# Where the gating branch and the front of the first head pair stand in a two-layer hybrid RWKV-7 / gMLP step

## The chip, the core and the metric

The kernel runs on one core of a Trainium2 chip. The metric is the time of one execution on the device, in microseconds: 3382.55, the median of three runs (3381.95 to 3396.24). TensorE multiplies matrices, VectorE and ScalarE work on elements, GpSimd (POOL in the profile) takes some element work, and SyncE (SP) issues all transfers, in order, from one queue. Every engine takes its own instructions in the order in which the program has them.

## What is computed

Two layers work on 640 tokens: 128 of a context and 512 of a latent grid, each with its own modulation. Of one layer, cut to what matters:

```python
z = h @ p['w_in'][l]                       # h: the normed, modulated input
z_rwkv, z_u, z_v, z_ga, z_gb = jnp.split(z, ...)
z_rwkv = z_rwkv + mu_shift * (shift_fn(z_rwkv) - z_rwkv)
y_a, S_fin = rwkv_branch(z_rwkv, S0, p, l)     # r, k, v, decay and a from lora; recurrence over tokens
# gating branch
u = jax.nn.gelu(z_u); v = jax.nn.gelu(z_v)
v = (v - mu) * lax.rsqrt(var + EPS) * p['ln_v_g'][l]
s = jnp.einsum('hpq,bnqhc->bnphc', p['w_s'][l], vc) + b_s     # mixes the tokens of a chunk of 128
y_b = (u * s) @ p['w_branch_b'][l]
mixed = (sigmoid(z_ga) * y_a + sigmoid(z_gb) * y_b) @ p['w_out'][l]
x = x + g1 * mixed                         # then a feed-forward block, gated by g2
```

The recurrence has 16 heads in two directions, `S = S * w + (S @ -kk) b^T + v k^T` and `y = S r`. `mod = silu(cond) @ w_ada` gives the shifts, scales and gates (48 columns of 128 channels a layer).

## The kernel before

Activations stand channel-major, 128 channels by 640 tokens. A product with fp32 weights is three passes of a split into `hi` and `lo`; a **dense block** (`dense`) makes 128 output channels: two loads of weights (`load_w`: `raw` by SP, `hi` on ScalarE, `lo` on VectorE, or by turns on GpSimd where `engs` says so) and 48 matmuls of 320 columns (line 111).

A layer runs in these stages:

- `n1`: the norm and the three lora blocks; their results are shifted by `shift_mix` (a copy to `zraw`, six transfers into the one tile `zs`, a mix on VectorE).
- `p1`, **the gating branch**, in a pool of its own: four token-major quarters of `z_v` (line 491), 40 lora units (line 463) that write the recurrence's inputs to `ld` in HBM, eight channel-major dense blocks of `z_u` (line 505, gelu, kept in `uts`), and `spatial` (line 443), which mixes tokens per head with weights and biases loaded whole at the start. In layer 0 the 32 late modulation columns (`mod_col`, line 168: a load of 512 KB and two VectorE reductions) stand between the dense blocks.
- `rw`, **the recurrence**, pair by pair of heads. `krv_block` makes k, r and v of a pair. `front(i)` prepares pair i: the normed key (`kksq` with Ln and Exp), for each direction the decays' running sums and their exponentials (`cum`, `E`), scaled copies `LA` and `BK`, Gram matmuls `g` (line 644), transposes, and a substitution of 30 steps on VectorE (lines 676 and 678). `back(i)` runs ten steps that depend on each other: matmuls on the state `SV`, a copy to `psb` on ScalarE, matmuls, copies back to `SV` on ScalarE and VectorE, sums on VectorE; then a group norm with Ln and Exp.
- The loop over pairs writes `back(i)` and `front(i+1)` interleaved, with the k, r, v blocks of the next pairs and **gate blocks** (the 16 dense blocks of `z_ga` and `z_gb`, spilled to HBM in `gd`) as fillers. The table `SP` says how many: `g0` within the front of pair 0, `gn[i]` around the end of pair i. `front(0)` runs ahead of the loop with only k, r, v of pairs 0 and 1 and a few gate blocks beside it.
- Then `branch_b`, which loads u * s from `bd`, and `p3` and `ff`, which do the rest.

A scheduler turns this into one fixed order per engine; `front` is written under a raised priority (`F`: 200), `back` under none. `pre` loads a ScalarE table that has Ln and Exp both, once, where the `rw` pool opens; `lnexp` asks only that an instruction stands behind it.

Of the kernel before, what the change touches and what calls it, by code (L numbers as in the profile page):

```python
# [6 lines left out]
F32 = mybir.dt.float32  # L7
# [27 lines left out]
SP = {'n': (3, 2, 1, 2, 2, 1, 0, 0, 3, 1), 'v': 1, 'k': 4, 'r': 7, 'kk': 7, 'F': 200, 'B': None, 't': 10, 'g0': 2, 'gn': (2, 2, 2, 1, 2, 2, 2, 1)}  # L35
# [6 lines left out]
def emit(tc, I, O, depth=DEPTH, mark=lambda s: None):  # L42
    nc = tc.nc
    ctx = ExitStack()
    with ctx:
# [117 lines left out]
        def mod_col(l, j, scr):  # L163
            wt = scr.tile([128, DM], F32, tag="wada", name="wada", bufs=2)
# [117 lines left out]
        yd = dram.tile([NK, 128, T], F32, name="yd")  # L282
        bvd = dram.tile([NPAIR, 128, T], F32, name="bvd")
# [23 lines left out]
        for l in range(depth):  # L307
# [73 lines left out]
            with tc.tile_pool(name=f"com{l}", bufs=1) as com:  # L381
# [10 lines left out]
                mark("p1")  # L392
                with tc.tile_pool(name=f"p1_{l}", bufs=1) as p1:
                    lah = p1.tile([128, 3, T], F32R, tag="lah", name="lah")
                    lal = p1.tile([128, 3, T], F32R, tag="lal", name="lal")
                    late = iter(range(16, 48 if l == 0 else 16))
                    if l == 0:
                        silu_c(p1)

                    def mod_some(n):  # L400
                        for _, j in zip(range(n), late):
                            mod_col(0, j, p1)

                    for j in range(3):
                        mod_some(0)
                        if l == 0:
                            ps = zps[j]
                        elif j < 2:
                            if j == 0:
                                pss = dense_pair(wsrc(I["win"][l, 24]), wsrc(I["win"][l, 25]), hh, hl)  # L410
                            ps = pss[j]
                        else:
                            ps = dense(I["win"][l, 24 + j], hh, hl)
                        t = p1.tile([128, T], F32, tag="pt", name="lz", bufs=4)
                        shift_mix(ps, 24 + j, t, l, com, cnt)
                        if j == 0:
                            nc.scalar.activation(t, t, AF.Tanh)
                        elif j == 2:
                            nc.scalar.activation(t, t, AF.Tanh, scale=0.5)
                            nc.vector.tensor_scalar(t, t, 0.5, 0.5, ALU.mult, ALU.add)  # L420
                        split(lah[:, j], lal[:, j], t)
                    stat = p1.tile([128, 5, 4], F32, tag="stat", name="stat")
                    vts = [p1.tile([128, DM], F32, tag=f"v{tk}", name=f"v{tk}") for tk in range(5)]
                    uts = p1.tile([128, NK, T], F32, tag="u", name="u")
                    bs_bc = p1.tile([128, NK, 128], F32, tag="bsb", name="bsb")
                    nc.sync.dma_start(bs_bc, I["bs"][l:l + 1].to_broadcast([128, NK, 128]))
                    wst = p1.tile([128, NK, 128], F32, tag="wst", name="wst")
                    nc.sync.dma_start(wst, I["wsT"][l])
                    turn = [0]

                    def halves_ps():
                        turn[0] += 1
                        if turn[0] % 2:
                            t = dense_ps()
                            return [t[:, n] for n in range(2)]
                        tag = ("g", "pu")[turn[0] // 2 % 2]
                        return [psr.tile([128, 512], F32, tag=tag, name="hps") for _ in range(2)]

                    def spatial(h):
                        ps = halves_ps()  # L440
                        for tk in range(5):
                            o = ps[tk // 4][:, (tk % 4) * 128:(tk % 4) * 128 + 128]
                            nc.tensor.matmul(o, vts[tk][:, h * 128:(h + 1) * 128], wst[:, h, :], start=True, stop=True)
                        st = p1.tile([128, T], F32, tag="st", name="st", bufs=3)
                        bsv = bs_bc[:, h, :].unsqueeze(1)
                        nc.vector.scalar_tensor_tensor(st[:, 0:512].rearrange("p (a t) -> p a t", a=4), ps[0].rearrange("p (a t) -> p a t", a=4),
                                                       P[:, LVG + h:LVG + h + 1], bsv.to_broadcast([128, 4, 128]), ALU.mult, ALU.add)
# [28 lines left out]
                    def lora(n):  # L476
                        for _ in range(n):
                            if next(units, 0) == 0:
                                break
# [598 lines left out]
```

## Time and profile before

| | us |
|---|---|
| median of three runs | 3382.55 |
| the profiled execution | 3388.05 |
| its span | 3386.3 |
| TensorE busy (matmuls / weight loads) | 3159.4 / 2862.3 |
| VectorE, ScalarE, GpSimd busy | 2145.6, 1511.6, 612.4 |

Times of the profile are from the span's start. "Busy" of TensorE counts a matmul until its modelled end, so matmuls that wait out their latency count too. The granted clock is a share of 2.4 GHz; 0.5 is the lower of its two levels, 1.2 GHz, and what lies between is a stretch with both. The program has no stage marks; the stretches below are cut at the first evacuation of the lora blocks (72.9 and 1742 us), near the end of the gating branch (262 and 1945), and at the first and last `psb` of a layer.

### The profile page before, as it was taken

Reading aid. Unit: us, or ns where it says so; the run is one execution under the profiler, and the core shown is the slowest. Engines: PE = TensorE matmul, PEld = TensorE weight load, DVE = VectorE, ACT = ScalarE, POOL = GpSimd, SP = SyncE. Lnnn points to the kernel's source line nnn. Section 1 sums busy time; section 2 is a strip of 40 time slices with the busy share of each in tenths; the row PEclk is TensorE's granted clock in tenths of the full one; section 3 lists DMA queues with packets and bytes.
Section 4 is the critical chain, followed back from the end, with each engine's and each line's share of the span. In section 5 each row is a group of like instructions: output and inputs, shape, how many; then the busy total and the mean of one; then the engine's idle time right before and its main releaser. Section 6 shows DMA issues by size and latency. Waiting matters only on the chain.

```text
span 3386.3 us, 66312 instructions
## 1 busy us (share of the span) xinstructions
PE 3159.4 (93%) x26160; PEld 2862.3 (85%) x26160; DVE 2145.6 (63%) x4147; ACT 1511.6 (45%) x3268; POOL 612.4 (18%) x616
## 2 busy tenths in 40 slices
PE   7998899999999999999989979999999999999998
PEld 7897677777778989999989967777777789899998
DVE  7777778887785469933353487788787735532234
ACT  5444445554445354224254434445544543541432
POOL 3004333333231000000000133333323210000000
PEclk8998889998899999999999989899889999999999
DMA  6683112221224536622344522122222245222223
GB/s 210 220 291 102 56 61 72 77 74 61 66 77 138 199 104 205 216 83 75 99 135 139 188 75 66 56 73 77 68 68 72 86 137 184 84 76 75 75 75 106
DMA packets 215671, 372.73 MB, mean 110 GB/s; under 512 B 63680, under 2 KB 72000, under 8 KB 215360
## 3 DMA queue, kind: packets, MB, share of 16 engines
q1 hardware_dynamic: 215360, 368.49, 33.8%
q8 instruction: 206, 3.38, 0.4%
q14 instruction: 105, 0.86, 0.1%
HBM read 288.41 MB, written 63.31 MB: 104 GB/s over the span
## 4 chain that ended last, share of the span: by engine, by line
PE 65%; DVE 18%; DMA 5%; issue 5%; ACT 4%; POOL 3%; SPq 1%; DVEq 0%; ACTq 0%; POOLq 0%
PE dps L111 40%; PE g L644 4%; DMA wada<-in_wada 3%; PE dps L256 3%; PE dps L491 2%; DVE X L678 2%; DVE D L676 2%; PE pu L776 2%; DVE wjunk L168 2%; PE pu L757 2%; PE pu L789 1%; PE pu L795 1%; PE pu L751 1%; DVE lo L103 1%; POOL BK L625 1%
## 5 line engine op out<-in xcount | busy, mean ns | idle before, releaser
L101 ACT ACTIVATE hi<-raw 128x512 fp32r<-128x512 f32 x630 | 397.2, 632 | 1025.6 <-PE dps L111 864.0
L103 DVE TENSOR_TENSOR lo<-raw,hi 128x512 fp32r<-128x512 f32 x550 | 392.1, 714 | 545.9 <-ACT hi L101 526.7
L111 PE MATMUL dps<-ah,hi 128*128 128x320 f32 x2768 | 686.9, 324 | 8.4 <-ACT up L468 5.4
L111 PE MATMUL dps<-ah,lo 128*128 128x320 f32 x2768 | 674.3, 321 | 14.5 <-DVE lo L103 14.5
L111 PE MATMUL dps<-al,hi 128*128 128x320 f32 x2768 | 674.9, 321 | 0.0
L111 PEld LDWEIGHTS dps<-ah,lo 128*128 128x128 f32 x2768 | 474.4, 193 | 29.5 <-DVE lo L103 16.5
L111 PEld LDWEIGHTS dps<-ah,hi 128*128 128x128 f32 x2768 | 474.2, 192 | 28.2 <-ACT up L468 6.0
L111 PEld LDWEIGHTS dps<-al,hi 128*128 128x128 f32 x2768 | 473.9, 192 | 12.7 <-issue 0.8
L168 DVE CUSTOM_DVE_ANT_0 wjunk<-wada,sc 128x1024 f32<-128x1024 f32 x176 | 220.9, 1255 | 33.2 <-DMA wada<-in_wada 30.9
L785 POOL TENSOR_TENSOR sw<-SV,wc 64x128 f32<-64x128 f32 x288 | 150.7, 523 | 439.0 <-DVE SV L803 422.5
L644 PE MATMUL g<-LA,BK 64*128 64x128 f32 x1280 | 193.6, 332 | 32.9 <-DVE LA L656 15.9
L103 POOL TENSOR_TENSOR lo<-raw,hi 128x512 fp32r<-128x512 f32 x80 | 123.2, 1540 | 543.6 <-ACT hi L101 491.8
L644 PEld LDWEIGHTS g<-LA,BK 64*128 64x128 f32 x1280 | 162.0, 226 | 64.6 <-issue 22.2
L111 PE MATMUL dps<-fh,lo 128*128 128x320 f32 x896 | 205.5, 311 | 6.2 <-DVE lo L103 6.0
L111 PE MATMUL dps<-fh,hi 128*128 128x320 f32 x896 | 204.7, 310 | 0.0
L111 PE MATMUL dps<-fl,hi 128*128 128x320 f32 x896 | 204.5, 309 | 0.0
L676 DVE TENSOR_TENSOR D<-AA,X 128x30 f32<-128x30 f32 (+14 forms) x480 | 178.1, 371 | 21.6 <-POOL X L671 11.7
L678 DVE TENSOR_TENSOR X<-X,D 128x30 f32<-128x30 f32 (+14 forms) x480 | 179.9, 375 | 11.3
L249 POOL TENSOR_TENSOR al<-nt,ah 128x320 fp32r<-128x320 f32 x24 | 25.2, 1053 | 728.1 <-ACT ah L248 727.0
L111 PEld LDWEIGHTS dps<-fh,lo 128*128 128x128 f32 x896 | 150.0, 188 | 7.9 <-DVE lo L103 7.8
L625 POOL TENSOR_TENSOR BK<-ta,cum 64x640 f32<-64x640 f32 x64 | 125.8, 1966 | 141.4 <-DVE ta L616 116.3
L111 PEld LDWEIGHTS dps<-fh,hi 128*128 128x128 f32 x896 | 150.3, 188 | 0.0
(293 smaller groups left out, 5798.1 us busy)
## 6 DMA issues: line engine op xcount, KB each, us to landing
raw<-in_w SPq DMA_DIRECT2D x280, 256.0 KB, 2.6
raw<-in_win SPq DMA_DIRECT2D x234, 256.0 KB, 2.7
wada<-in_wada SPq DMA_DIRECT2D x88, 512.0 KB, 4.1
ld<-up SPq DMA_DIRECT2D x80, 320.0 KB, 3.6
th<-ld SPq DMA_DIRECT2D x32, 320.0 KB, 2.9
ta<-ld SPq DMA_DIRECT2D x32, 320.0 KB, 3.0
gd<-spill SPq DMA_DIRECT2D x32, 320.0 KB, 2.3
raw<-in_wo SPq DMA_DIRECT2D x40, 256.0 KB, 2.6
```

What stands on the lines that cost most here:

```text
L101: nc.scalar.activation(hi, raw, AF.Copy)
L103: (eng or nc.vector).tensor_tensor(lo, raw, hi.bitcast(F32), ALU.subtract)
L111: nc.tensor.matmul(ps[:, n, 0:HT], w[:, k * 128:(k + 1) * 128], xk[:, n * HT:(n + 1) * HT], start=(first and k == 0 and j == 0), stop=(las ...
L168: nc.vector.tensor_tensor_reduce(junk, wt, sc_cur[0][:, v, :], 1.0, 0.0, ALU.mult, ALU.add, mods[l][:, j, v:v + 1])
L256: nc.tensor.matmul(ps[:, n, 0:HT], w[:, k * 128:(k + 1) * 128], x[:, 4 * kb + k, hs(n)], start=(kb == 0 and k == 0 and j == 0), stop=(kb = ...
L491: nc.tensor.matmul(o, x[:, k, tk * 128:(tk + 1) * 128], w[:, kk * 256:(kk + 1) * 256], start=(k == 0 and j == 0 and tk % 2 == 0), stop=(k ...
L625: nc.gpsimd.tensor_tensor(b[s, c, 1 - h, :], rt[s], e[s], ALU.mult)
L644: nc.tensor.matmul(gs[h][:, c - c0, :], b[s, c, :, :].rearrange("p x t -> p (x t)"), la[s, c, h:h + 2, :].rearrange("p x t -> p (x t)"), s ...
L676: nc.vector.tensor_tensor(t3, AA[:, s + 1:32, s:s + 1].to_broadcast([128, n, s]), X[:, s:s + 1, 0:s].to_broadcast([128, n, s]), ALU.mult)
L678: nc.vector.tensor_tensor(X[:, s + 1:32, 0:s], X[:, s + 1:32, 0:s], t3, ALU.add)
L757: nc.tensor.matmul(pu[s, d, 3, :], SV[:, us[d], h, :], GR[d][:, cs[d], h, :], start=False, stop=True, skip_group_check=True)
L785: nc.gpsimd.tensor_tensor(sw[s], SV[s, both, h, :], wcu[s, both].unsqueeze(2).to_broadcast([64, 2, L]), ALU.mult)
```

## The change

- The pool `rw` now opens ahead of the gating branch, and so `pre` and the fronts stand ahead of it too; the tiles of odd pairs (`LA2`, `TT1` and their like) move to a pool `rwb` that takes the gating branch's room after it.
- k, r and v of pair 0 come right behind the lora inputs; half the lora units follow, and then the steps of `front(0)` are written between the quarters of `z_v`, the remaining lora units and `spatial`.
- The eight `z_u` blocks become fillers like the gate blocks: stored raw to `zud` in HBM, read back in pair 7, where gelu and the product with s are taken (`branch_b_prep`). `gn` grows from 14 to 22 fillers. `spatial` stores s alone.
- `spatial` loads its weights and bias head by head into tiles of two buffers. Lora weights are loaded half by half across the three kinds.
- The 32 modulation columns of layer 0 move to the odd steps of the pairs, with one buffer for their load.
- The scratch of dynamic transfers is made smaller (2048 bytes), which is SBUF room.

```diff
-SP = {..., 'g0': 2, 'gn': (2, 2, 2, 1, 2, 2, 2, 1)}
+SP = {..., 'g0': 2, 'gn': (2, 3, 3, 3, 3, 3, 3, 2)}
...
+                            pool = odd[0] if name in ("LA2", "LA3", "BK2", "BK3", "GR2", "GR3", "TT1") else rw
...
-                    gates = [(x, m) for x in range(2) for m in range(8)]
+                    fillers = [(27 + m, zud[m]) for m in range(8)] + [(43 + 8 * x + m, gd[x, m]) for x in range(2) for m in range(8)]
...
-                    wst = p1.tile([128, NK, 128], F32, tag="wst", name="wst")
-                    nc.sync.dma_start(wst, I["wsT"][l])
...
+                        krv(0, 0, 1, 2)
...
+                        def spatial(h):
+                            ws = p1.tile([128, 128], F32, tag="wst", name="wst", bufs=2)
+                            nc.sync.dma_start(ws, I["wsT"][l, :, h])
+                            bs = p1.tile([128, 128], F32, tag="bsb", name="bsb", bufs=2)
...
+                        lora(20)
+                        run(0, 5)
+                        for q in range(4):
...
+                            lora(5)
+                            run(0, 3)
...
+                        krv(1, 0, 1)
+                        for h in range(NK):
+                            run(0, 2)
+                            spatial(h)
+                        run(0)
...
-                        for m in range(NK):
+                    def branch_b_prep(m):
+                            bh, bl = bb["h"], bb["l"]
                             t = tmp("bs", "ta", 2)
                             nc.sync.dma_start(t, bd[m])
+                            u = ftmp("u")
+                            nc.sync.dma_start(u, zud[m])
+                            nc.scalar.activation(u, u, AF.Gelu_apprx_tanh)
+                            nc.vector.tensor_tensor(t, t, u, ALU.mult)
                             split(bh[m], bl[m], t)
...
+                        for i in range(NPAIR):
...
+                                if step % 2:
+                                    mod_some(1)
+                                if i == NPAIR - 1:
+                                    if step == 0:
+                                        branch_b_tiles()
+                                    if step < NK:
+                                        branch_b_prep(step)
```

On TensorE, where the first Gram matmuls of pair 0's front (`g`) stand: before, between dense blocks (`dps` from `ah`, `al`) behind the gating branch.

```order
L111 MATMUL dps<-ah,lo 128x320 x2
L111 MATMUL dps<-ah,hi 128x320 x2
L111 MATMUL dps<-al,hi 128x320 x2
L644 MATMUL g<-LA_2793,BK_2794 128x128 x8
L111 MATMUL dps<-ah,lo 128x320 x2
L111 MATMUL dps<-ah,hi 128x320 x2
L111 MATMUL dps<-al,hi 128x320 x2
L111 MATMUL dps<-ah,lo 128x320 x2
```

There pair 0's front has only dense blocks beside it. In the changed program, still on TensorE:

```order
L833 MATMUL dps<-lo,ah 128x256
L833 MATMUL dps<-hi,al 128x256
L833 MATMUL dps<-hi,ah 128x256
L518 MATMUL g<-LA_1148,BK_1149 128x128 x8
L833 MATMUL dps<-hi,ah 128x256
L833 MATMUL dps<-lo,ah 128x256
L833 MATMUL dps<-hi,al 128x256
L833 MATMUL dps<-lo,ah 128x256
L833 MATMUL dps<-hi,al 128x256
```

They stand now between token-major matmuls of `z_v` (line 833), inside the gating branch.

On ScalarE, in the loop's first pairs, the end of the key's norm of a later pair (`kksq`), between copies of the recurrence (`psb`, `SV`). Before:

```order
L587 ACTIVATE kksq<-k,par_163 128x640
L790 ACTIVATE SV<-pu 64x2x64
L101 ACTIVATE hi<-raw 128x512
L293 ACTIVATE zraw<-dps 128x640
L553 ACTIVATE kksq<-pg,c_e_98 128x320
L294 ACTIVATE r<-dps,dpar_165 128x640
L553 ACTIVATE kksq<-pg,c_e_98 128x320
L553 ACTIVATE kksq<-kksq 128x640
L780 ACTIVATE psb<-pu 128x128
L790 ACTIVATE SV<-pu 64x2x64
```

No table load stands there. In the changed program, at the same place:

```order
L461 ACTIVATE kksq<-k,par_164 128x640
L295 ACTIVATE r<-dps,dpar_166 128x640
L654 ACTIVATE psb<-pu 128x128
L664 ACTIVATE SV<-pu 64x2x64
L427 ACT_TABLE_LOAD
L427 ACTIVATE kksq<-pg,c_e_98 128x320 x2
L427 ACT_TABLE_LOAD
L427 ACTIVATE kksq<-kksq 128x640
L101 ACTIVATE hi<-raw 128x512
L654 ACTIVATE psb<-pu 128x128
```

A table load stands ahead of the Ln (`kksq` from `pg`) and another ahead of the Exp; the group norm's Ln and Exp have the same two.

On VectorE, in the substitution of a pair (`D`, `X`) beside the recurrence of the pair before (`SV`). Before:

```order
L678 TENSOR_TENSOR X<-X,D 128x24x7
L676 TENSOR_TENSOR D<-AA,X 128x184
L678 TENSOR_TENSOR X<-X,D 128x23x8
L791 COPY SV<-pu 64x2x64
L676 TENSOR_TENSOR D<-AA,X 128x198
L678 TENSOR_TENSOR X<-X,D 128x22x9
L803 TENSOR_TENSOR SV<-pu,sw 64x2x64
L676 TENSOR_TENSOR D<-AA,X 128x210
L803 TENSOR_TENSOR SV<-pu,sw 64x2x64
```

The substitution shares the queue with the recurrence alone there. In layer 0 of the changed program, the same place (the rows named ISA are a modulation column's reduction and its read):

```order
L638 TENSOR_TENSOR YD<-pu,YD 128x64
L552 TENSOR_TENSOR X<-X,D 128x12x19
L638 TENSOR_TENSOR YD<-pu,YD 128x64
L550 TENSOR_TENSOR D<-AA,X 128x220
L665 COPY SV<-pu 64x2x64
L552 TENSOR_TENSOR X<-X,D 128x11x20
L168 ISA wjunk,mod_171<-wada,sc 128x1024
L168 ISA mod_171 128x1
L550 TENSOR_TENSOR D<-AA,X 128x210
L677 TENSOR_TENSOR SV<-pu,sw 64x2x64
```

One reduction after the other stands between two steps of the substitution and ahead of a sum into `SV`.

## Rows read from the trace of the kernel before

**Rows 1.** Windows by stage: A:B length, busy us of each engine (instructions), PEclk, DMA share, GB/s

```profile
core 0: us, PE busy (x) PEld busy (x) DVE busy (x) ACT busy (x) POOL busy (x), PEclk, DMA share, GB/s
72.90:262.00 189.10, 176.87 (x1285) 170.37 (x1286) 137.87 (x232) 89.50 (x180) 6.79 (x13) 0.98 0.76 252
262.00:378.90 116.90, 88.86 (x683) 80.04 (x682) 93.90 (x149) 53.59 (x119) 45.29 (x29) 0.82 0.27 82
378.90:1074.30 695.40, 649.82 (x6742) 529.74 (x6741) 536.12 (x1181) 342.26 (x909) 226.57 (x240) 0.92 0.24 75
1074.30:1170.00 95.70, 95.28 (x652) 93.28 (x651) 43.59 (x69) 40.16 (x62) 0.00 (x0) 1.00 0.59 197
1742.00:1945.00 203.00, 197.60 (x1438) 192.13 (x1437) 73.42 (x114) 97.57 (x189) 11.04 (x16) 0.98 0.47 161
1945.00:2046.10 101.10, 73.74 (x588) 65.55 (x589) 82.66 (x137) 44.86 (x105) 40.84 (x26) 0.80 0.25 78
2046.10:2743.80 697.70, 651.47 (x6743) 530.94 (x6743) 537.56 (x1181) 342.48 (x909) 223.96 (x240) 0.92 0.24 75
```

**Rows 2.** Tile `psb`: ns min/median/max, first and last start in us

```profile
L780 ACT ACTIVATE psb<-pu x160: 250/278/297, 378.9 to 2743.8; 128x128 f32<-128x128 f32 x160
```

**Rows 3.** Windows of pairs of layer 0, first `psb` to next pair's first

```profile
656.30:740.00 83.70, 80.50 (x889) 64.69 (x888) 69.27 (x159) 45.30 (x122) 27.20 (x30) 0.98 0.24 72
740.00:855.00 115.00, 102.33 (x958) 85.22 (x959) 91.03 (x182) 51.98 (x136) 40.25 (x38) 0.84 0.22 70
...
1036.30:1074.30 38.00, 38.00 (x453) 29.91 (x453) 21.02 (x49) 18.75 (x47) 8.47 (x14) 1.00 0.53 168
```

**Rows 4.** Windows: between pairs 0 and 1; steps of pair 3; between pairs 3 and 4

```profile
431.10:465.10 34.00, 30.51 (x343) 26.87 (x344) 31.34 (x49) 19.75 (x41) 12.16 (x8) 0.90 0.20 61
656.30:721.30 65.00, 62.77 (x616) 50.11 (x617) 54.89 (x140) 29.58 (x89) 23.92 (x27) 0.97 0.22 68
721.30:740.00 18.70, 17.73 (x277) 14.59 (x275) 14.38 (x20) 15.72 (x34) 3.28 (x3) 1.00 0.29 87
```

**Rows 5.** Windows of 5 us between the last step of pair 0 and pair 1

```profile
445.00:450.00 5.00, 1.66 (x53) 1.39 (x53) 5.00 (x6) 2.95 (x5) 0.89 (x2) 0.83 0.30 117
450.00:455.00 5.00, 5.00 (x99) 4.61 (x97) 3.51 (x4) 2.63 (x6) 3.17 (x2) 0.50 0.17 56
...
460.00:465.00 5.00, 4.89 (x42) 3.50 (x42) 5.00 (x5) 4.82 (x13) 3.86 (x2) 1.00 0.27 86
```

**Rows 6.** Window of 50 us in layer 0's feed-forward, dense blocks alone

```profile
1450.00:1500.00 50.00, 50.00 (x343) 50.00 (x342) 13.01 (x24) 10.94 (x17) 0.00 (x0) 1.00 0.25 77
```

**Rows 7.** Groups by line: count | busy us, mean ns | idle before it and what ended it

```profile
L101 ACT ACTIVATE hi<-raw 128x512 fp32r<-128x512 f32 x630 | 397.2, 632 | 1025.6 <-PE dps L111 864.0 <-PE dps L491 48.3 <-PE dps L256 46.9
...
L168 DVE CUSTOM_DVE_ANT_0 wjunk<-wada,sc 128x1024 f32<-128x1024 f32 x176 | 220.9, 1255 | 33.2 <-DMA wada<-in_wada 30.9
...
L678 DVE TENSOR_TENSOR X<-X,D 128x30 f32<-128x30 f32 (+14 forms) x480 | 179.9, 375 | 11.3
L676 DVE TENSOR_TENSOR D<-AA,X 128x30 f32<-128x30 f32 (+14 forms) x480 | 178.1, 371 | 21.6 <-POOL X L671 11.7
...
L692 DVE STREAM_TRANSPOSE XT<-X 128x1024 f32<-128x1024 f32 x16 | 32.2, 2011 | 0.3
...
L168 DVE DVE_READ_ACCUMULATOR2_ANT mod<- 128x1 f32 x176 | 14.4, 82 | 0.0
```

**Rows 8.** Timeline of ScalarE behind pair 7: start, us taken, instruction [idle before]

```profile
1079.49 0.74 ACT L820 ACTIVATE YD<-yc 128x640 f32<-128x640 f32 x1 [1.56 <-DVE yc L818]
1080.24 1.28 ACT L553 ACT_TABLE_LOAD   x1
1081.54 0.95 ACT L553 ACTIVATE YD<-pg,c_gn 128x320 f32<-128x320 f32 x2
```

**Rows 9.** Tile `st`, ns min/median/max; transfers, KB each and median us to landing

```profile
L446 DVE SCALAR_TENSOR_TENSOR st<-dps,par,bsb x8: 744/747/753, 183.7 to 1914.0; 128x512 f32<-128x512 f32 x8
...
bd<-st SPq DMA_DIRECT2D x16, 320.0 KB, 2.7
```

More of the change, by code (lines that the diff above doesn't have):

```diff
@@ L161, in mod_setup, with mod_col @@
             mods[l] = G([128, 48, 2], f"mod{l}")
-        def mod_col(l, j, scr):
-            wt = scr.tile([128, DM], F32, tag="wada", name="wada", bufs=2)
+        def mod_col(l, j, scr, bufs=2):
+            wt = scr.tile([128, DM], F32, tag="wada", name="wada", bufs=bufs)
             nc.sync.dma_start(wt, I["wada"][l, j])
@@ L563, in krv_block, with spill_block @@
                         shift_mix(ps, blk, out, l, com, cnt)
-                    def gate_block(x, m):
-                        ps = dense(I["win"][l, 43 + 8 * x + m], hh, hl, engs=(None, nc.gpsimd))
+                    def spill_block(blk, dst):
+                        ps = dense(I["win"][l, blk], hh, hl, engs=(None, nc.gpsimd))
                         t = ftmp("spill")
                         nc.scalar.activation(pv(t), ps[:, :, 0:HT], AF.Copy)
-                        nc.sync.dma_start(gd[x, m], t)
+                        nc.sync.dma_start(dst, t)
                     def ch(t):
@@ L854, in gate @@
                         nonlocal gi
-                        for _ in range(min(n, len(gates) - gi)):
+                        for _ in range(min(n, len(fillers) - gi)):
                             mark("gate")
-                            gate_block(*gates[gi])
+                            spill_block(*fillers[gi])
                             gi += 1
@@ L868, in branch_b, with branch_b_tiles @@
+                    bb = {}
+                    def branch_b_tiles():
                         sp = []
@@ new lines, in emit, with mod_some @@
+                    with tc.tile_pool(name=f"rwb{l}", bufs=1) as rwb:
+                        odd[0] = rwb
+                        late = iter(range(16, 48 if l == 0 else 16))
+                        if l == 0:
+                            silu_c(rwb)
+                        def mod_some(n):
+                            for _, j in zip(range(n), late):
+                                mod_col(0, j, rwb, 1)
+                        b = back(0)
+                        adv(b, "B", 0)
+                        gate(SP["g0"])
+                        run(1, 5)
+                        for i in range(NPAIR):
+                            ng = SP["gn"][i]
+                            for step in range(10):
+                                adv(b, "B", i)
+                                run(i + 1, SP["n"][step])
+                                if step % 2:
[5 more added lines that the diff above has]
+                                        branch_b_prep(step)
+                                if step == SP["v"]:
+                                    krv(i + 1, 2)
+                                if step == SP["k"]:
+                                    krv(i + 2, 0)
+                                if step == SP["r"]:
+                                    krv(i + 2, 1)
+                                if step == SP["kk"]:
+                                    run(i + 2, 1)
+                            gate(ng if i == NPAIR - 1 else min(ng, 1))
+                            if i == NPAIR - 1:
+                                if l == 0:
+                                    mod_late(0)
+                                ya = new_acts()
+                                for j in range(NPAIR - 1):
+                                    t = ftmp("ya")
+                                    nc.sync.dma_start(t, yd[j])
+                                    split(ya[0][:, j], ya[1][:, j], t)
+                            drain(b, "B", i)
+                            if i == NPAIR - 1:
+                                branch_b()
+                            gate(ng - 1)
+                            run(i + 1)
+                            if i + 1 < NPAIR:
+                                b = back(i + 1)
+                                adv(b, "B", i + 1)
+                            run(i + 2, 4)
```

264 lines of the change are left out of this document (100 added, 164 removed).

## The prediction

> **What bounds the kernel now.** I read the stretches of the program first: for each layer the gating branch, the front of pair 0 that stands alone behind it, the loop over the eight pairs, and what follows [rows 1]. The loop's ends are the first and the last `psb` of a layer [rows 2]. Layer 0's gating branch takes 189.1 us with TensorE busy for 176.9; then the front of pair 0 takes 116.9 us with only 88.9 busy, at a granted clock of 0.82; layer 1 repeats this with 203.0 (197.6) and 101.1 (73.7, clock 0.80). So 40 us of layer 0 and 33 us of layer 1 are idle TensorE ahead of the loop, most of it in pair 0's front, a chain on VectorE that has too little beside it. In the loop TensorE looks full (649.8 of 695.4 us), yet weight loads are busy for only 529.7 [rows 1]: a small matmul of the recurrence counts as busy while it waits out its latency. VectorE is at 536 of 695. No engine is the bound there: it is a chain through TensorE, ScalarE and VectorE, each taking its queue in order. Its pace shows in the pairs: the last pair, with no front beside it, takes 38.0 us for its ten steps, where others take 84 to 115 us each [rows 3]; the mean over seven pairs is (1036.3 - 378.9) / 7 = 93.9 us.
>
> The sum is made on the profiled execution, 3388.05 us, 5.5 above the median of the runs, 3382.55; at the end the 5.5 comes off.
>
> **Term 1: ahead of the loop.** A dense block is 48 matmuls; where nothing else runs, 343 of them take 50 us [rows 6], 0.146 us each, 7.0 us a block. Counted in the two programs' orders, 17 blocks besides the token-major half and the lora units stand ahead of the loop before, and 7 after: ten blocks, 70 us a layer, leave. TensorE's busy time there is 176.9 + 88.9 = 265.8 us in layer 0; without the ten it is 195.8, and if the two fronts of work really overlap, that is nearly all that is left. Two new waits come. First, pair 0's substitution now runs beside the token-major blocks, which need their `lo` halves from the same VectorE queue: before the last three of these, eleven substitution steps (0.371 + 0.375 us each [rows 7]) and two transposes (2.0 us each [rows 7]) stand in a row, some 12 us, against a few us of matmuls ready; I take 12 us. Second, `spatial` loses its preloaded weights and biases to pairs of small tiles: every two heads wait for VectorE's two `st` (0.75 us each for the larger part [rows 9]), for a transfer (2.7 us to landing for the nearest, `bd` [rows 9]) and an issue queue in order; about 6 us for 2 us of matmuls, four times, so 15 us. Against that, the 0.82 means that about 42 us of 117 ran at the lower clock (1.2 GHz), which can lose 21; with TensorE kept busy I take 15 back. Layer 0: 306.0 becomes 195.8 + 27 - 15 = 208; layer 1: 304.1 becomes 271.3 - 70 + 12 = 213. **Gain 98 + 91 = 189 us.** Ends: 140, if only the blocks leave and all the idle time stays, and some 215.
>
> **Term 2: the same blocks in the loop.** Between the first step of pair 0 and that of pair 7 there are 398 more dense matmuls in layer 0 and 386 in layer 1: 784 x 0.146 = 114 us. What is paid? In the changed order a middle pair has 162 to 165 of them inside its steps and 110 to 124 between its last step and the next pair's first. Pairs with 151 to 158 inside exist already: pair 3 takes 65.0 us for its steps, and 18.7 us to the next pair with 42 matmuls there [rows 4]. Between pairs 0 and 1 stand 105, and that takes 34.0 us, of which 3.3 are idle and 5 at half the clock [rows 4, 5]; twenty more would fill those first. So a pair becomes 66 + 34 = 100 us; with the shorter pairs of the changed order (251, 279 and 197 matmuls: about 90, 99, 85) seven pairs are 674 us in place of 657: **+17 a layer, 34 in all.** Ends: 114, and below zero, since the loop's clock of 0.92 [rows 1] stands for about 110 us per layer at half rate (pair 4: 0.84 and 115 us [rows 3]). Another 143 matmuls land behind pair 7, where TensorE is busy for 95.3 of 95.7 us [rows 1]: **+21**, in full. Their transfers cost nothing: what `hi` waits for is TensorE (864 of 1025.6 us), not its `raw` [rows 7]. The second path of `zu` through HBM, and gelu and product in pair 7, lie in the emptiest pair (VectorE 21.0 of 38.0 [rows 3]).
>
> The Trainium skill, Perfetto Trace Analysis, Identifying the Most-Contended Engine, says matmul busy time is a poor measure of headroom, and weight-load busy time a good one. By matmul busy time the loop has 46 us of room per layer and a rule of thumb would charge most of the 114 (the sum below would become +36); by weight-load time it has 166 and all would fit (the sum -78). The pairs in the trace lie nearer to the second.
>
> **Term 3: table loads, which the diff doesn't show.** `pre` loads the table with both Ln and Exp once; before, it stands behind the gating branch. Now tanh and gelu of that branch run after it, so the order has a load ahead of each Ln and each Exp group: four per pair, 60 in the two loops. One takes 1.28 us, and the next instruction starts 1.30 us after it, as the end of layer 0 already shows [rows 8]: 78 us of ScalarE. Two of the four stand in the last steps, between copies of the recurrence (`psb`, `SV`); two among the copies that open the next pair, where ScalarE is already busy for 4.8 of 5 us [rows 5]. I take half, **+39**; ends 10 and 78.
>
> The Trainium skill, ScalarE: Activation LUTs, What ACT_TABLE_LOAD costs, adds a drain of about 1.38 us to each switch. By it the 60 would be 160 us, and half of that would take the sum to -3. The trace shows no such drain: the load starts at the end of the instruction ahead of it [rows 8].
>
> **Term 4: the modulation columns of layer 0.** Thirty-two of them, each two reductions of 1.255 us and two reads of 0.082 [rows 7], go from the gating branch (where TensorE was near full in any case, so nothing is won there) to the steps of pairs 0 to 6: 64 x 1.337 = 86 us of VectorE, ten reductions per pair. About three of ten stand where VectorE waits; the others lie between substitution steps and the recurrence's `SV` copies and sums. Pair 3 has VectorE busy for 69.3 of 83.7 us [rows 3]; 13.4 more would nearly fill it. I take 60%, **+51**; ends 20 and 86. The next column's load waits on SP for the one buffer; behind it queue weight blocks, which have slack [rows 7], and the shifts. I charge nothing more, and it would be part of the 86.
>
> **Sum:** -189 + 34 + 21 + 39 + 51 = -44. 3388 - 44 = 3344; on the median, **3339 us**.
>
> **The rivals.** *Slower: the recurrence's chain pays every insertion.* Place: steps 0 to 9 of each pair, on the queues of ScalarE and VectorE. Loads and columns in full are 78 + 86 = 164 in place of 90: -189 + 34 + 21 + 164 = +30, 3413 us. For it: both queues are in order and the chain goes through both. Against it: neither is full (ScalarE 342, VectorE 536 of 695 [rows 1]). It decides from 134 of the 164 on. *Faster still: the fill keeps the clock.* Blocks in the loop cost nothing and 30 us of half-rate time come back: -108, 3275 us. For it: the low clock follows slices in which TensorE idled (1.66 of 5 us busy, then 0.50 [rows 5]). Against it: the waits that idle TensorE between a pair's scaling on VectorE and its Gram matmuls stay. *It doesn't do what it says: pair 0's front and the branch take turns.* The order puts front matmuls between the branch's, but in order on one queue each can wait for the other's VectorE work; then term 1 is 140 and the sum +5, 3388 us.
>
> **How the numbers follow.** Forecast 0.5, slower chain 0.2, kept clock 0.15, taking turns 0.15. The ends of the terms around the forecast give about 60 us down and 75 up; with the rivals the range is 3265 to 3415. A measurement can tell about 0.5% (17 us) from no change, so the marks are 3366 and 3399. Faster: most of the forecast, all of the kept clock and a little of the third: 0.63. Same: 0.16. Slower: 0.21.
>
> **What would show it.** From the first evacuation of the lora inputs to the first `psb`: 208 and 213 us; over 230 says that they took turns. Layer 1's loop, which has no columns: about 735 us; near 700 says that the blocks were free, over 770 that they and the loads were paid. Layer 0's loop less layer 1's: about 50 us is the columns' price. The page should show some 90 table loads. The prediction is wrong if layer 0's loop passes 860 us, or if layer 1's does not grow.

## The result and the profile after

The changed kernel takes 3586.89 us, the median of four runs (3573.73 to 3597.73), against 3382.25 for the kernel before: 1.059 times as long (95% interval 1.055 to 1.064). The forecast was 3339 us, with 3265 to 3415 as its range. The profiled execution took 3588.89 us; its span is 3587.1.

The stages of the changed kernel, cut as in [rows 1] (length, busy us of each engine with instructions, granted clock, share of the transfers):

```profile
72.80:334.30 261.50, 220.48 (x1478) 197.95 (x1478) 128.83 (x217) 127.47 (x271) 35.90 (x36) 0.84 0.38 128
334.30:1133.30 799.00, 733.65 (x7162) 602.57 (x7159) 634.75 (x1332) 396.15 (x967) 253.66 (x253) 0.91 0.31 97
1133.30:1230.00 96.70, 96.70 (x666) 95.34 (x663) 43.36 (x68) 42.36 (x66) 0.00 (x0) 1.00 0.64 212
1810.80:2080.30 269.50, 230.36 (x1557) 206.59 (x1555) 135.06 (x220) 129.16 (x272) 40.60 (x33) 0.85 0.37 125
2080.30:2931.70 851.40, 794.28 (x7137) 628.39 (x7139) 567.51 (x1194) 393.83 (x961) 233.84 (x251) 0.88 0.23 72
```

| stage, us | before | after | change | forecast |
|---|---|---|---|---|
| layer 0, ahead of the loop | 306.0 | 261.5 | -44.5 | -98 |
| layer 0, loop | 695.4 | 799.0 | +103.6 | +88 |
| layer 1, ahead of the loop | 304.1 | 269.5 | -34.6 | -91 |
| layer 1, loop | 697.7 | 851.4 | +153.7 | +36 |
| both layers behind the loop, and the start | 1383.1 | 1405.7 | +22.6 | +21 |

Two things stand out. Ahead of the loops under half of the expected time was won. And layer 1's loop, which has no modulation columns, grew more than layer 0's, which has all of them.

**Layer 1's loop.** Its middle pairs repeat every 128 us (first `psb` of pairs 3 to 6 at 2415.3, 2543.4, 2671.4 and 2799.4). In each there is a stretch like this one, on TensorE (start, us taken, instruction, count):

```profile
2498.08 0.64 PE L111 MATMUL dps<-al,hi 128*128 128x320 f32 x1
2498.65 0.31 PE L589 MATMUL pw<-XT,XN 32*32 32x32 f32 x2
2498.89 0.64 PE L111 MATMUL dps<-ah,lo 128*128 128x320 f32 x1
2499.45 0.31 PE L589 MATMUL pw<-XT,XN 32*32 32x32 f32 x2
```

One dense matmul, one small one (the records count a small one twice), one dense, one small: a round takes 0.81 us, longer than five dense matmuls where nothing else runs (0.146 each by [rows 6]). In the kernel before, the same group of `pw` stood together:

```profile
2492.03 1.78 PE L705 MATMUL pw<-XN,TT 32*32 32x32 f32 x80 [1.28 <-DVE XN L694]
...
2497.91 2.35 PE L715 MATMUL pw<-XT,XN 32*32 32x32 f32 x80
```

Over layer 1's loop I counted in the trace 118 stretches of dense matmuls between `pw` after, with 141 matmuls in 67 us, against 2 before; `pw` itself takes 54 us against 24. The clock is low all through such a stretch, though TensorE counts as busy without a gap; this is the window from 2484 to 2514 us:

```profile
2484.00:2514.00 30.00, 30.00 (x170) 18.83 (x170) 2.58 (x7) 4.30 (x10) 2.06 (x3) 0.51 0.11 34
```

**Ahead of the loop** TensorE is idle for 41.0 us in layer 0 and 39.1 in layer 1; before it was 40.3 and 32.8 [rows 1]. In all, none of it is gone. Ten blocks left, but the lower clock took some of that back: 0.84 over 261.5 us means 84 us at half rate in layer 0, and 0.98 and 0.82 before [rows 1] mean 50. Where the idle time lies (engine, what it does and waits for, us, times, longest):

```profile
PE dps L804 <- ACT v L837: 8.7, 3, 6.8
PE dps L804 <- ACT up L809: 8.6, 7, 5.1
PE dps L786 <- DMA wst<-in_wsT: 8.2, 3, 3.7
PE dps L833 <- DVE lo L103: 3.1, 5, 1.3
```

The longest of these, on ScalarE, where instructions of pair 0's front (`E`, `cum`) and of the branch (`v`) stand in one queue:

```profile
151.82 0.74 ACT L427 ACTIVATE E<-cum 128x640 f32<-128x640 f32 x1 [4.90 <-DVE cum L480]
152.58 1.28 ACT L837 ACT_TABLE_LOAD   x1
153.87 0.38 ACT L837 ACTIVATE v<-dps 128x256 f32<-128x256 f32 x1
154.28 1.28 ACT L427 ACT_TABLE_LOAD   x1
155.57 0.74 ACT L427 ACTIVATE cum<-cum 128x640 f32<-128x640 f32 x1
156.32 1.28 ACT L837 ACT_TABLE_LOAD   x1
157.62 1.21 ACT L837 ACTIVATE v<-dps 128x256 f32<-128x256 f32 x4
```

The evacuation of `v` waits behind `E`, which waits 4.90 us for VectorE's `cum`, and three table loads of 1.28 us lie in 5 us, since `v` takes gelu and `E` takes Exp. TensorE's next matmul has waited 6.80 us:

```profile
158.61 0.90 PE L804 MATMUL dps<-lah,hi 64*128 64x320 f32 x2 [6.80 <-ACT v L837]
```

### The profile page after: what moved, and what is told of

Read it like the earlier page. It is cut to its first block, busy times and chain, and to the rows that moved or that the text cites. A ratio compares the mean times of both kernels' runs of the same rounds, so it can differ in the third digit from the quotient of the medians.

```text
span 3587.1 us, 66505 instructions
## 1 busy us (share of the span) xinstructions
PE 3319.9 (93%) x26160; PEld 2950.6 (82%) x26160; DVE 2159.9 (60%) x4131; ACT 1600.4 (45%) x3346; POOL 625.3 (17%) x632
## 4 chain that ended last, share of the span: by engine, by line
PE 68%; DVE 16%; ACT 6%; issue 4%; DMA 4%; POOL 1%; SPq 1%; DVEq 0%; POOLq 0%; ACTq 0%
PE dps L111 45%; PE g L518 4%; PE dps L833 2%; PE dps L256 2%; DVE wjunk L168 2%; DVE D L550 2%; DVE X L552 2%; DVE lo L103 2%; PE pu L631 2%; PE pu L650 2%; PE pw L589 2%; PE pu L663 2%; DMA wada<-in_wada 1%; PE pg L452 1%; PE pu L669 1%
## 5 line engine op out<-in xcount | busy, mean ns | idle before, releaser
L111 PE MATMUL dps<-ah,lo 128*128 128x320 f32 x2768 | 707.4, 331 | 32.1 <-DVE lo L103 31.2
L111 PE MATMUL dps<-ah,hi 128*128 128x320 f32 x2768 | 707.4, 332 | 5.2 <-ACT hi L101 2.0
L111 PE MATMUL dps<-al,hi 128*128 128x320 f32 x2768 | 709.2, 331 | 0.0
L111 PEld LDWEIGHTS dps<-ah,lo 128*128 128x128 f32 x2768 | 484.8, 196 | 53.2 <-DVE lo L103 35.1
L111 PEld LDWEIGHTS dps<-ah,hi 128*128 128x128 f32 x2768 | 483.1, 196 | 25.1 <-ACT hi L101 4.2
L111 PEld LDWEIGHTS dps<-al,hi 128*128 128x128 f32 x2768 | 485.9, 196 | 18.8 <-issue 0.4
L168 DVE CUSTOM_DVE_ANT_0 wjunk<-wada,sc 128x1024 f32<-128x1024 f32 x176 | 229.6, 1305 | 17.4 <-DMA wada<-in_wada 15.5
L103 POOL TENSOR_TENSOR lo<-raw,hi 128x512 fp32r<-128x512 f32 x96 | 138.9, 1447 | 408.7 <-ACT hi L101 248.4
L518 PE MATMUL g<-LA,BK 64*128 64x128 f32 x1280 | 177.6, 312 | 21.4 <-DVE LA L530 9.8
L518 PEld LDWEIGHTS g<-LA,BK 64*128 64x128 f32 x1280 | 150.4, 209 | 46.4 <-issue 30.4
```

Of the source, the lines that this page charges most:

```text
L103: (eng or nc.vector).tensor_tensor(lo, raw, hi.bitcast(F32), ALU.subtract)
L111: nc.tensor.matmul(ps[:, n, 0:HT], w[:, k * 128:(k + 1) * 128], xk[:, n * HT:(n + 1) * HT], start=(first and k == 0 and j == 0), stop=(las ...
L518: nc.tensor.matmul(gs[h][:, c - c0, :], b[s, c, :, :].rearrange("p x t -> p (x t)"), la[s, c, h:h + 2, :].rearrange("p x t -> p (x t)"), s ...
```

## The experiments

Eleven of the twelve kernels that ran are timed against the kernel before, and one is read from its trace alone. Stage lengths in the table are those of each profiled execution, in us; it can lie up to 18 us from the median (e6's is the furthest, above it).

| kernel | ahead, layer 0 | loop, layer 0 | ahead, layer 1 | loop, layer 1 | median |
|---|---|---|---|---|---|
| changed | 261.5 | 799.0 | 269.5 | 851.4 | 3586.9 |
| e1: `pw` together | 252.9 | 829.3 | 259.3 | 777.6 | 3520.2 |
| e2: e1 + table again | 248.8 | 806.4 | 260.8 | 769.9 | 3487.3 |
| e3: e1 + blocks back | 293.2 | 753.3 | 306.5 | 732.1 | 3478.6 |
| e4: e1, no columns | 252.2 | 777.6 | 256.5 | 777.2 | 3464.2 |
| e6: e2 + blocks back | 293.3 | 766.5 | 304.6 | 710.2 | 3445.8 |
| e7: e2 + buffers | 234.6 | 808.9 | 248.5 | 772.9 | 3458.7 |
| e8: e6 + buffers, columns written later | 290.5 | 756.8 | 305.9 | 716.0 | 3445.9 |
| e9: e2, front behind | 301.7 | 784.7 | 278.4 | 765.6 | 3532.3 |
| e11: e6, no columns | 298.4 | 712.9 | 301.8 | 709.2 | 3409.5 |
| e12: before, no columns | 290.2 | 694.0 | 308.3 | 688.5 | 3362.7 |
| e13: changed, no columns | 261.3 | 861.1 | 269.7 | 844.9 | 3638.5 |

**e1: `pw` together.**

```diff
-    nc.tensor.matmul(pw[x][...], A21[...], XN[...], start=True, stop=True)
+    with tc.high_priority(offset=1000):
+        nc.tensor.matmul(pw[x][...], A21[...], XN[...], start=True, stop=True)
```

(and the same for the second group.)

> The changed kernel with one thing added: the 80 small matmuls of each of a pair's two `pw` groups (32x32, lines 579 and 589) are written under a raised priority, so that they stand together on TensorE as in the kernel before (32 stretches of `pw` in the program against 262 in the changed kernel). Theory A (alternation): layer 1's loop, 851.5 us in the changed kernel, is long because single dense matmuls stand between pairs of `pw`. There, 118 stretches of dense matmuls between `pw` hold 141 matmuls and take 67 us (141 x 0.146 = 21 if they stood together), and `pw` itself takes 54 us against 24 before; that is 46 + 30 = 76 us, so layer 1's loop becomes 765 to 785, layer 0's 785 to 799 (its own extra is 15 us), the total about 3490. Theory B (the blocks are paid wherever they stand, by TensorE at half its clock): the alternation only fills time that TensorE would have waited, layer 1's loop stays above 825 and the total above 3560.

3520.23 us, 1.0375 of before (1.0351 to 1.0399). The two loops:

```profile
326.10:1155.40 829.30, 756.43 (x7168) 625.08 (x7166) 644.32 (x1335) 397.27 (x968) 256.29 (x253) 0.87 0.29 94
2092.50:2870.10 777.60, 697.70 (x7152) 578.53 (x7150) 578.96 (x1196) 390.95 (x962) 230.15 (x251) 0.95 0.25 79
```

Layer 1's loop is 74 us shorter, at a clock of 0.95 in place of 0.88: theory A. Of its 118 stretches 2 are left, with 11 matmuls. Layer 0's loop did not follow; it grew by 30, and the total fell by 67 rather than 97. In that loop the clock fell from 0.91 to 0.87: some 216 us at half rate in place of 144, which is worth 36 us, so the 30 us can all lie in the clock. Its pairs 2 and 3 take 79 and 94 us for their ten steps, where the changed kernel took 71 and 67; there Gram matmuls `g` alternate with lone dense ones (681 to 690 us). No run here shows whether that lowered it.

**e13: the changed kernel without columns.** The call of `mod_some` in the steps is dropped, and constants stand in for the columns; nothing else is changed.

> The changed kernel as it is, without the 32 modulation columns in layer 0's loop (left out, constants in their place) and with nothing done about `pw`. Without them the program of layer 0's loop has the same alternation of `pw` and single dense matmuls as layer 1's: 201 stretches of `pw` in the first half of TensorE's order, against 66 in the changed kernel (196 in the second half in both). Theory A (alternation): taking work away makes layer 0's loop longer, 851 as in layer 1 in place of 799, and the total about 3635. Theory B (work is paid where it stands): the loop loses the columns' 52 us, 747, and the total is about 3535.

3638.54 us, 1.0742 (1.0712 to 1.0771): leaving work out made the kernel 52 us slower. Layer 0's loop:

```profile
333.90:1195.00 861.10, 802.86 (x7161) 636.62 (x7161) 571.81 (x1201) 396.39 (x966) 235.78 (x253) 0.87 0.22 71
```

It is layer 1's loop again (851.4 us, 794.28 busy), and the trace has layer 1's alternation in it: 118 stretches with 147 dense matmuls between `pw`, where the changed kernel's layer 0 has 22 with 61. Theory A forecast 3635; theory B, 3535. Less work took longer, in another order.

**e10: the alternation by itself.** Behind the kernel before, on constant tiles, in a fixed order:

```diff
+        big(200); small(240); big(240)
+        for _ in range(120):
+            big(1)
+            small(2)
+        big(120)
```

> The kernel before with a measurement behind its end, in a fixed order on TensorE, from constant tiles: 200 dense matmuls (128x320), 240 small ones (32x32) together, 240 dense, then 120 times one dense and two small by turns, then 120 dense. Together, 120 dense and 240 small should take 17.5 us (0.146 each) and 5 us (80 in 1.7 us in the loop before). Theory A (a change between the two shapes costs by itself): the 120 rounds take 62 us if the clock stays full (0.52 a round, as the trace of the changed kernel shows at 2482 us) and 97 if it falls (0.80, as at 2500 us). Rival (only the clock matters): the rounds take 23 us at full and 46 at half clock.

Again the records count a small matmul twice. Stretches first (200 big; 240 small; most of the rounds), then the rounds as they begin and as they end:

```profile
3367.00:3396.00 29.00, 29.00 (x200) 29.00 (x199) 6.06 (x12) 1.00 (x2) 0.00 (x0) 1.00 0.13 46
3396.40:3408.00 11.60, 9.19 (x481) 8.98 (x480) 0.00 (x0) 0.00 (x0) 0.00 (x0) 0.81 0.02 4
3450.00:3539.00 89.00, 89.00 (x550) 51.59 (x549) 0.00 (x0) 0.00 (x0) 0.00 (x0) 0.50 0.00 1
```

```profile
3444.66 0.25 PE L1043 MATMUL small<-sm 32*32 32x32 f32 x4
3444.84 0.42 PE L1037 MATMUL big<-bx,bw 128*128 128x320 f32 x1
3445.18 0.25 PE L1043 MATMUL small<-sm 32*32 32x32 f32 x4
3445.36 0.42 PE L1037 MATMUL big<-bx,bw 128*128 128x320 f32 x1
...
3538.28 0.64 PE L1037 MATMUL big<-bx,bw 128*128 128x320 f32 x1
3538.84 0.32 PE L1043 MATMUL small<-sm 32*32 32x32 f32 x4
3539.09 0.64 PE L1037 MATMUL big<-bx,bw 128*128 128x320 f32 x1
...
3539.90 2.50 PE L1037 MATMUL big<-bx,bw 128*128 128x320 f32 x8
```

Two hundred big ones take 29.66 us (from 3366.71) and 240 small ones 11.70 (3396.37 to 3408.07), of which TensorE is idle for 2.4 us and partly at half clock. The first 122 small ones ran at full clock without a break:

```profile
3396.37 4.05 PE L1043 MATMUL small<-sm 32*32 32x32 f32 x244
```

So 120 and 240 take 17.8 + 11.7 = 29.5 us together, or 17.8 + 8.0 = 25.8 at the pace of that row. (The 5 us expected for the small ones took 80 records for 80 matmuls.) By turns they take 3539.90 - 3444.66 = 95.2 us. The first rounds, at full clock, take 0.52 us, the last 0.81; the loop's rounds, with one small matmul in place of two, take the same. So it is both: a round would be 0.246 us (or 0.215) without the changes of shape, so that each of its two changes costs 0.14 us (or 0.15); and the clock falls, in spite of an engine that counts as busy throughout. The big matmuls are also of type fp32r and the small ones of fp32, and no run here separates type from shape. The Trainium skill, TensorEngine Tiling (Array Packing), Tiling Modes, says that changing the tiling mode, not only the tile, drains TensorE. The trace agrees, as far as shape is what costs: 128x128 and 32x32 by turns cost 0.14 us per change at full clock.

**e2: the table again.**

```diff
-    pre = tc.keep_in_program_order(nc.scalar.preload_act_table_set("natural_log_exp_and_others"))
+    pre = [tc.keep_in_program_order(nc.scalar.preload_act_table_set("natural_log_exp_and_others"))]
...
+    pre[0] = tc.keep_in_program_order(nc.scalar.preload_act_table_set("natural_log_exp_and_others"))
     b = back(0)
```

> e1_pw_together with the table that has both Ln and Exp loaded once more behind the gating branch, so that the loops hold no reloads (37 table loads in the program in place of 93). The prediction's term: half of 78 us, so 39 less than e1 in all, about 20 in each loop. Rival, the chain pays each load in full: 78 less, 39 in each loop. Rival, the loads are hidden: within 10 us of e1.

3487.32 us (1.0283, 1.0264 to 1.0301), 33 below e1. The group of the loads, in the changed kernel and in e2:

```profile
L427 ACT ACT_TABLE_LOAD x70 | 89.8, 1283 | 3.2 <-PE pg L452 2.0
```

```profile
L427 ACT ACT_TABLE_LOAD x12 | 15.4, 1283 | 0.2
```

The group is as large in e1. In all, e1's trace has 93 loads and e2's 37: 56 fewer, 72 us less of ScalarE, of which 33 showed in the time. Layer 0's loop is 23 shorter, layer 1's 8.

**e3 and e6: the blocks back in the branch**, without and with the table.

```diff
-    'gn': (2, 3, 3, 3, 3, 3, 3, 2)
+    'gn': (2, 2, 2, 1, 2, 2, 2, 1)
...
-    lora(20)
+    for m in range(5):
+        lora(4)
+        gate(1)
     run(0, 5)
...
     lora(5)
+    if q < 3:
+        gate(1)
     run(0, 3)
```

> e1_pw_together with the eight channel-major blocks of z_u written into the gating branch again, beside the lora units and the quarters of z_v (still stored raw and read back in pair 7), and the loop's numbers of fillers as before (2,2,2,1,2,2,2,1). If dense blocks in the loop cost what the prediction took (17 us a layer), the loops become 17 us shorter each and the time ahead of the loop 7 us a block longer, 56 a layer, less what a fuller TensorE gives back in clock: the total is 0 to 80 us above e1. If instead the loop pays the blocks in full or at half clock while the branch had waits that they fill (TensorE waited some 40 of 261 us there and ran 85 at half clock), each loop becomes 50 to 70 us shorter and the time ahead of it at most 35 longer: the total is 30 to 70 us below e1.

> e3_blocks_back and e2_table_again together: the z_u blocks in the gating branch, the table loaded again behind it, `pw` kept together. If the costs add, it is 33 us below e3 (3479), as e2 was below e1, so about 3446: layer 0's loop 753 to 730, layer 1's 732 to 724. What is left against the kernel before would then be the columns in layer 0's loop (52 us by e4 against e1). If the loads delay the chain more where fewer blocks fill the loop, the gain is up to 78.

3478.64 (1.0261, 1.0237 to 1.0285) and 3445.84 us (1.0176, 1.0145 to 1.0207): 42 and 41 us below e1 and e2, and the costs of blocks and table add. By stages of e1 and e3 the loops are 76 and 46 us shorter, the stretches behind them 11 and 8, and the time ahead 40 and 47 longer. Of the eight blocks some seven leave each loop (339 and 326 fewer dense matmuls in the trace, 49 and 48 us at 0.146): layer 1's loop had paid about their full price and layer 0's more (from e2 to e6 it is the other way, 40 and 60 us), while eight blocks (56 us) lengthened the time ahead by less than that. In e3 TensorE hardly waits for `up` in layer 0's branch (0.6 us, against 11 in the changed kernel), and the granted clock there is 0.96 in place of 0.84: the blocks were what stood beside the lora units.

**e4: no columns**, on e1. The call of `mod_some` is dropped, with constants in place of the columns.

> e1_pw_together without the 32 modulation columns in layer 0's loop (left out, with constants in their place). The prediction's term: layer 0's loop is 51 us shorter than in e1. Rival, paid in full: 86 us shorter. Rival, hidden in VectorE's waits: under 20. Without them the two layers' loops run the same program, so they should then agree within 10 us.

3464.17 us (1.0214, 1.0196 to 1.0232). Layer 0's loop:

```profile
324.60:1102.20 777.60, 702.03 (x7170) 584.34 (x7165) 581.96 (x1203) 393.47 (x967) 232.60 (x253) 0.94 0.25 80
```

It is 52 us shorter and now equals layer 1's (777.2). The clock rose from 0.87 to 0.94: 93 us at half rate in place of 216, worth 61 us. TensorE's idle time did not fall (75.6 us, and 72.9 in e1). So what the columns cost there shows in the clock, and not in longer waits of TensorE; how they lower it no run here shows.

**e12 and e11: no columns in the kernel before, and in e6.** In both the tanh that prepares their input is dropped too, which e4 and e13 keep.

> The kernel before without the 32 columns in layer 0's gating branch (left out in the same way). The prediction took them for free there, since TensorE was near full: within 10 us of the kernel before. Rival, their reductions on VectorE or their 16 MB on the transfer queue hold the branch up: 20 to 50 us less.

> e6_blocks_back_table without the 32 modulation columns and without the loads and tanh they need (left out, constants in their place): of the change there remain the front of pair 0 between the parts of the gating branch, the raw z_u with its gelu and product in pair 7, and weights of spatial by heads. If the costs found so far are all there is (columns 52 and up to 15 for their tanh ahead of pair 0), it takes 3446 - 60 = about 3385 and is within 15 of e12_before_no_columns: the interleaving wins nothing where the blocks stand beside it. If the front really overlaps, as the prediction took it, it is 30 to 60 below e12.

e12: 3362.73 us (0.9933, 0.9912 to 0.9953), 20 to 24 below the kernel before, 16 of it ahead of layer 0's loop. In the branch the columns, with their tanh, were not free. e11: 3409.47 us (1.0057, 1.0032 to 1.0082), so 47 above e12, where at most 15 were expected. Layers 0 and 1 ahead of their loops, e11 first:

```profile
72.50:370.90 298.40, 254.29 (x1878) 233.58 (x1878) 136.22 (x226) 137.90 (x294) 50.98 (x47) 0.95 0.39 131
1749.90:2051.60 301.70, 265.90 (x1940) 243.62 (x1938) 138.56 (x228) 138.78 (x292) 51.86 (x42) 0.95 0.40 135
```

```profile
72.70:362.90 290.20, 259.00 (x1966) 246.06 (x1967) 152.44 (x245) 139.37 (x295) 52.21 (x42) 0.93 0.39 136
1722.50:2030.70 308.20, 273.76 (x2028) 259.46 (x2027) 159.42 (x250) 142.47 (x294) 48.75 (x41) 0.91 0.38 132
```

Ahead of the loops e11 takes 600.1 us in all and e12 598.4, although two dense blocks a layer (28 us) moved into e11's loops; TensorE's idle time there is 44.1 and 35.8 us against 31.2 and 34.4. Interleaved with the blocks beside it, pair 0's front won nothing (e11 also has the new `spatial` and lora loads, which these two kernels do not separate). The loops are 19 and 21 longer: the two blocks (some 14 us), and pair 7, whose ten steps take 46.6 and 43.8 us in place of 38.2 in layer 0 of e12, now that gelu, product and reloads of z_u stand in it.

**e9: pair 0's front behind the branch**, on e2.

```diff
-    run(0, 5)
...
-    run(0, 3)
...
-    krv(1, 0, 1)
     for h in range(NK):
-        run(0, 2)
         spatial(h)
+    run(0, 17)
+    krv(1, 0, 1)
     run(0)
```

> e2_table_again with pair 0's front written behind the gating branch again and not between its parts (k, r and v of pair 0 still come first, the z_u blocks are still fillers of the loop); k and r of pair 1 come in the midst of it. It measures the interleaving alone, ahead of the loop, where e2 takes 248.8 and 260.8 us. By the prediction's overlap, pair 0's front (117 and 101 us with 28 us of idle TensorE and a low clock before) would stand alone again with less beside it, so 35 to 60 us longer in each layer, the total 70 to 120 above e2. By the rival that branch and front take turns (TensorE's idle time ahead of the loop is 40 us before and 41 after in layer 0, 33 and 41 in layer 1): within 15 us in each layer.

3532.28 us (1.0435, 1.041 to 1.046), 45 above e2. Ahead of the loops, e9:

```profile
73.40:375.10 301.70, 223.01 (x1526) 202.34 (x1526) 152.89 (x251) 127.00 (x269) 46.79 (x40) 0.81 0.37 127
1835.30:2113.70 278.40, 225.64 (x1544) 205.06 (x1543) 120.85 (x201) 120.55 (x256) 33.88 (x28) 0.83 0.35 120
```

Layer 0 is 53 us longer and layer 1 18; the loops give 26 back. Idle TensorE is 78.7 and 52.8 us, against 44.9 and 42.2 in e2. Part of the shift is work that moved: 52 more dense matmuls and twelve more column reductions stand ahead of layer 0's loop than in e2, and 31 more dense matmuls ahead of layer 1's; the 45 us in all count both sides. So with the blocks gone the interleaving does work. It fills the holes that the leaving blocks made.

**e7: more buffers**, on e2: `pt` 3 to 5, `wst` and `bsb` 2 to 3.

> e2_table_again with more buffers in the gating branch: five for the evacuated lora units (`pt`) in place of three, three for the weights and biases of `spatial` in place of two. Ahead of layer 0's loop TensorE waited in the changed kernel some 13 us for `up` and 8 for `wst`, and ran 85 us at half clock. Theory buffers: these waits are for room, so the time ahead of each loop falls by 12 to 25 us (248.8 and 260.8 in e2), the total by 25 to 50. Theory order: the evacuations stand on ScalarE behind instructions of pair 0's front (`E`, `kksq`, `vp`) that wait for VectorE, so more room changes little: each within 8 us of e2.

3458.73 us (1.022, 1.0193 to 1.0247), 29 below e2; the time ahead of the loops is 14 and 12 us shorter, the low end of theory buffers. The waits of TensorE for ScalarE's `up` and `v` in layer 0's branch, e2 first, then e7:

```profile
PE dps L806 <- ACT up L811: 10.4, 6, 5.1
PE dps L806 <- ACT v L839: 8.7, 3, 6.8
```

```profile
PE hps L788 <- DMA wst<-in_wsT: 7.0, 2, 5.6
PE dps L806 <- ACT v L839: 5.7, 3, 3.8
...
PE dps L806 <- ACT up L811: 4.8, 4, 3.3
```

For `wst` TensorE waited 9.0 us in e2 and still 7.0 in e7. Both theories held a part.

**e8: columns written later**, on e6 with e7's buffers: one behind pairs 0 to 6 each, eight in pair 7, the others beside `branch_b`.

> e6_blocks_back_table with the buffers of e7 and with the 32 modulation columns of layer 0 moved out of the recurrence's steps: one behind the last step of each of pairs 0 to 6, eight beside the steps of pair 7, where VectorE has room, and the rest beside branch_b (VectorE 44 of 96 us there before). If the columns cost 52 us only where the chain meets them, layer 0's loop comes within 15 us of layer 1's and the stretch behind it grows by at most 15: about 40 below e6, near 3400. If the chip charges them wherever they stand, it gains under 15. Faster than the kernel before only if the interleaved front gains more than the 13 and -2 us that e3 showed ahead of its loops.

3445.91 us (1.0187, 1.0159 to 1.0215), as e6. The edit did not do what it was for: the scheduler took the columns, which wait for nothing but their load, forward again. In the trace all 64 reductions lie between 360 and 959 us, all but two inside layer 0's loop, as in e6 (362 to 1013). The buffers won next to nothing here either (290.5 and 305.9 us ahead of the loops, against 293.3 and 304.6 in e6). What columns behind the loop would cost was not measured, and no version here beats the kernel before with the whole computation in it.

## Why the prediction was wrong

One edit at a time leads from the changed kernel to the kernel before: 3587, `pw` together 3520 (-67), table again 3487 (-33), blocks back 3446 (-41), columns and their tanh out 3409 (-36), front and the rest of the change out 3363 (-47), columns back in the branch 3387 (+24). Of the 248 us between the forecast and the measured time, 110 lie ahead of the loops and 133 in them.

- **Missed: the order itself (-67).** Term 2 counted how many dense matmuls stand inside and between the steps, and took their price from pairs 0 to 3, where fillers and `pw` stand apart. It did not look at what stands next to what. The order of the changed program had it: 262 stretches of `pw` in place of 32, 196 of them in its second half. The step that failed is "so a pair becomes 66 + 34 = 100 us": in layer 1 it became 128, and 109 once `pw` stood together (e1's pairs 3 to 6). No rival had this mechanism either.
- **Term 2's price.** Forecast +17 us a layer for the blocks in the loop; e1 and e3 show 76 and 46, e2 and e6 40 and 60, for some seven blocks that take 49 or 48 alone. The upper end of 57 was near. The pairs it was taken from had idle time and low clock to fill only as long as few blocks came. The term weighed the rule of the Trainium skill, Perfetto Trace Analysis, Identifying the Most-Contended Engine, that weight-load time shows the room on TensorE, against the sum by matmul busy time, and judged the pairs to be nearer the rule. Here the measured price sides with matmul busy time. The term for the tail was right (+21; the stages behind the loops and the start grew by 22.6).
- **Term 1.** Forecast -189, measured -79, below the low end of 140. The assumption "nearly all that is left" is busy time failed: idle time stayed at 40 us, in waits for `up` and `v` that the term did not name, beside those it did (`lo` 3.1 of the 12 us, `wst` 8.2 of the 15). And the clock went the other way: 15 us were to come back; instead 34 more us at half rate cost 17. The rival in which front and branch take turns described this best, for part of it: over 230 us from the lora inputs to the first `psb`, here 261.5 and 269.5. e9 qualifies it. The front did overlap, and what it gained was lost by taking away the blocks.
- **Term 3 was right in its sum.** 91 table loads in the trace, and 33 us by e2 and again between e3 and e6, for a forecast of 39. By layers it was 23 and 8 in e2, not 20 each. The load starts where the instruction ahead of it ends (152.56 to 152.58 us in the rows above), so there is no drain here either.
- **Term 4 met its number once, by luck.** On e1 the columns cost 52 us in the loop (51 forecast). But the term was a share of VectorE's time that the recurrence waits out, and e4 shows a higher clock with TensorE's idle time unchanged. On e6 they cost 36, tanh included. In the changed kernel itself they saved 52 (e13): with them, layer 0's order has little of the alternation. That they cost nothing in the branch was wrong by some 20 us, tanh included.
- **The tests it set itself** were half useful: layer 1's loop over 770 did say "paid", but the difference of the loops (-52 in place of +50) was meant as the columns' price, and would have been misread without e4. Its two signs of being wrong, layer 0's loop over 860 us and layer 1's not growing, did not come.

Terms as measured at e1's order: -98 ahead (with the clock) + 122 blocks in the loops + 19 tails + 33 + 52 = +128, where e1 is 131 above the kernel before; the alternation adds 67 on top, +195, near the measured +204. The parts overlap, so the sum is not exact.

## What to carry to other kernels

Before a filler is costed by its count, read in the order what it will stand between: one large matmul between small ones of another tile shape and type cost a multiple of its own time here, at a clock that stayed low while the engine looked full. A scheduler's order can turn with an unrelated edit, so look at both halves of a program that should be alike. And when work is moved out of a stage, ask what waits it was covering there; the overlap that replaces it has first to fill those.

## What the runs showed of the hardware

- A dense 128x320 matmul (fp32r) and two 32x32 ones (fp32) by turns take 0.52 us at the full clock and 0.81 at half, against 0.215 to 0.246 together; 0.14 to 0.15 us per change (e10).
- The granted clock was 0.51 and 0.50 in stretches in which TensorE counts as busy for all of the time (30.00 of 30.00 us in the loop, 89.00 of 89.00 in e10). Its weight loads are busy for 18.83 and 51.59 us of those.
